# Seven block products for a seventh pair of row tiles, and low parts of the ordinary rows by an adding transfer

## The chip, the cores and the metric

The kernel runs on one core of a Trainium2 chip. The metric is the device time of one execution in microseconds (us). Three executions of the kernel before gave 928.75, 930.30 and 930.32 us; their median is 930.3 us.

## What is computed

A two-layer encoder over 256 tokens of width 1024. Each layer has a feed-forward block, a mixer (two kinds of attention, side by side) and a second feed-forward block, each behind a residual and a layer norm. The change lies in the second matrix product of the feed-forward block, which runs four times:

```python
def swiglu(x, w_in, w_out):                 # D_FF = 2816
    h = x @ w_in
    gate, up = h[..., :D_FF], h[..., D_FF:]
    return (jax.nn.silu(gate) * up) @ w_out
...
for l in range(DEPTH):                      # DEPTH = 2
    x = layer_norm(ALPHA * x + 0.5 * swiglu(x, ffn1_w_in[l], ffn1_w_out[l]), ...)
    x = layer_norm(ALPHA * x + hybrid_mixer(x, ...), ...)
    x = layer_norm(ALPHA * x + 0.5 * swiglu(x, ffn2_w_in[l], ffn2_w_out[l]), ...)
```

## The kernel before

**High and low parts.** Every float32 operand A is split into a high part Ah, rounded to the type fp32r, and a low part Al = A - Ah. A product is three matmuls: Ah·Bh, Ah·Bl and Al·Bh. For a weight row tile of 128x1024 (512 KB), SyncE issues the load into a tile `raw` (L116), ScalarE casts it to `wh` (L118), and VectorE subtracts to get `wl` (L119).

**Buffers and look-ahead.** `raw` has 5 buffers, `wh` and `wl` 9 each, and the general pool `tmp` 7. Buffers of one name are handed out in the order in which the program asks for them. `Weights.get(i)` (L126) asks for the rows ahead, up to nine slots; an ordinary row counts one slot and a pair four. TensorE's instructions run in the order of the program. The other engines' orders are planned at compile time by priority; the splitting work has a lower one (`LATER`).

**The two products of a feed-forward block.** The first makes 22 column tiles of the hidden layer, j = 0 to 21 (`col`, L404, from j = 4 on, mostly two at a time, four weight slots and about 11 us each time). The activations, split, lie in `gs[q]`, q = j // 2. The second product multiplies the 256 tokens (two tiles t = 0, 1) by 22 row tiles k of `w_out`. An ordinary row tile is a `step` (L496): for each t three parts by two column halves, 6 matmuls of 128x512; 12 for both t, and 24 for two row tiles. A pair q in `STR` takes row tiles 2q and 2q+1 as a two by two block matrix and spends seven block products, three matmuls each, 21 in all (`pair`, L507). For it, VectorE forms sums of the weights (L86 to L89: 2 loads in `raw`, a third `raw` for sums, and `t4` in `tmp`), and four splits follow, b, t, a and f (L90 to L93), each a cast (L72) and a subtraction (L73); f is half as wide. The activations' sums are formed in `sums` (L448) when column 2q+1 is done; `f` is a `tmp` tile for a short time, and the results of the first three pairs of `STR` lie in `xp` buffers, those of the others in two `tmp` tiles each, until the pair is through.

**The order of the second product.** `PLAN` gives its first part: six pairs and three ordinary rows, "o o S o S S S S S". Then the four sums of the pair products are folded into the residual (L541 to L550). Then comes the tail of `TAIL` = 7 ordinary rows: first all seven for t = 0 (L552), whose layer norm runs under the following seven for t = 1 (L563). The next stage's rows are loaded and split meanwhile.

**Names in the profile.** Rows have the number in the list of all loads; in the first feed-forward block of layer 0 the pairs are 46 and 48 to 52 (46a and 46b the loads, 46b, 46t, 46a, 46f the splits), the last pair is 52, and TensorE starts the second product at 128.08 us.

Of the kernel before, what the change touches and what calls it, by code (L numbers as in the profile page):

```python
# [9 lines left out]
F32 = mybir.dt.float32  # L10
F32R = mybir.dt.float32r
# [3 lines left out]
ALU = mybir.AluOpType  # L15
# [4 lines left out]
P = 128  # L20
# [4 lines left out]
JT = DFF // P  # L25
# [12 lines left out]
NB = 4  # L38
LATER = 100
WARM = 9  # L40
STR = (3, 4, 5, 6, 7, 8)
PLAN = "o o S o S S S S S"

# [14 lines left out]
class Weights:  # L60
# [15 lines left out]
    def _make_pair(self, i):  # L76
# [16 lines left out]
            (t4,) = self._halves(i, t4, "f")  # L93
        self.made.append((b11, b21, b22, t4, t1, t2, t3))

    def _slots(self, i):
        return 4 if self.srcs[i][0] == "S" else 1

    def _make(self, i):
        nc = self.nc  # L100
        if self.srcs[i][0] == "S":
            return self._make_pair(i)
        raw = self.pool.tile([P, 1024], F32, tag="raw", name=f"raw{i}", bufs=5)
        wh = self.pool.tile([P, 1024], F32R, tag="wh", name=f"wh{i}", bufs=9)
        wl = self.pool.tile([P, 1024], F32R, tag="wl", name=f"wl{i}", bufs=9)

        n = 512 if i < 3 else 1024
        src = self.srcs[i]

        rows = src if isinstance(src, tuple) else (src,)  # L110
        for c in range(0, 1024, n):
            s = slice(c, c + n)
            for q, r in enumerate(rows):
                h = P // len(rows)

                (nc.sync if i or c else nc.scalar).dma_start(raw[q * h : (q + 1) * h, s], r[:, s])  # L116
            with self.tc.high_priority(0 if i < 3 else -LATER):
                nc.scalar.copy(wh[:, s], raw[:, s])  # L118
                nc.vector.tensor_tensor(wl[:, s], raw[:, s], wh[:, s].bitcast(F32), ALU.subtract)  # L119
        self.made.append((wh, wl))  # L120
# [15 lines left out]
def encoder_kernel(  # L136
# [22 lines left out]
    nc = tc.nc  # L159
# [13 lines left out]

    singles = [k for k in range(JT) if k // 2 not in STR]
    singles, tail = singles[: len(singles) - TAIL], singles[len(singles) - TAIL :]
    plan, left, pairs = [], list(singles), list(STR)
    for u in PLAN.split():
        plan.append((u, (left if u == "o" else pairs).pop(0)))
    assert not left and not pairs

    def out_rows(w):
        row = lambda k: w[k * P : (k + 1) * P, :]
        rows = [row(k) if u == "o" else ("S", row(2 * k), row(2 * k + 1)) for u, k in plan]
        return rows + [row(k) for k in tail]

    srcs = []
    for l in range(DEPTH):
        srcs += [f1_b[l, k] for k in range(KT)]
        srcs += [f1_in[l, j, s] for j in range(JT - NB) for s in range(2)]
        srcs += out_rows(f1_out[l])  # L190
        for c in range(3):
            srcs += [m_in[l, c, q] for q in range(4)]
        srcs += [m_in2[l, q] for q in range(2)]
        srcs += [m_in[l, 3, q] for q in range(4)]
        srcs += [m_out[l, k * P : (k + 1) * P, :] for k in range(KT // 2)]

        srcs += [tuple(m_out[l, 512 + 256 * v + HD * n : 512 + 256 * v + HD * (n + 1), :] for v in range(2))
                 for n in range(KT // 2)]
        srcs += [f2_b[l, k] for k in range(KT)]
        srcs += [f2_in[l, j, s] for j in range(JT - NB) for s in range(2)]  # L200
        srcs += out_rows(f2_out[l])
# [5 lines left out]
    xx = cp.tile([P, KT, 2, 2, P], F32R, name="xx")  # L207
# [153 lines left out]
    def ffn(l, n, last=False):  # L361
# [42 lines left out]
        def col(*js, flip=False):  # L404
# [26 lines left out]
            for j, hs, tl, ws in ts:  # L431
                for s in range(2):
                    two(hs, ws, s)
                    nc.scalar.copy(tl[:, s], hs[s][:, 1, :])  # L434
                    dv.tensor_tensor(tl[:, s], hs[s][:, 0, :], tl[:, s], ALU.add)  # L435
                nc.scalar.activation(tl[:, 0], tl[:, 0], AF.Silu)  # L436
                gv = tl[:, 1]
                dv.tensor_tensor(gv, tl[:, 0], gv, ALU.mult)  # L438
                q, jj = divmod(j, 2)
                n = P if q in STR and jj == 0 else SEQ  # L440
                nc.scalar.copy(gs[q][:, jj, 0, 0:n], gv[:, 0:n])  # L441
                dv.tensor_tensor(gs[q][:, jj, 1, 0:n], gv[:, 0:n], gs[q][:, jj, 0, 0:n].bitcast(F32), ALU.subtract)
                if q in STR and jj:
                    sums(q, ts[0][2][:, 1], gv)
# [3 lines left out]
        def sums(q, g0, g1):  # L448

            f = tp.tile([P, 4, P], F32, tag="tmp", name=f"sf_{nm}_{q}")  # L450
            if STR.index(q) < 3:
                s = xp.tile([P, 2, 4, P], F32R, tag="x", name=f"s_{nm}_{q}")
                sh, sl = s[:, 0], s[:, 1]
            else:
                sh, sl = (tp.tile([P, 4, P], F32R, tag="tmp", name=f"s{c}_{nm}_{q}") for c in "hl")
            a11, a21, a12, a22 = g0[:, 0:P], g0[:, P:SEQ], g1[:, 0:P], g1[:, P:SEQ]
            dv.tensor_tensor(f[:, 0], a21, a22, ALU.subtract)
            dv.tensor_tensor(f[:, 1], a11, f[:, 0], ALU.subtract)
            dv.tensor_tensor(f[:, 2], a21, a11, ALU.subtract)
            dv.tensor_tensor(f[:, 3], a12, f[:, 1], ALU.subtract)  # L460
            nc.scalar.copy(sh, f)
            dv.tensor_tensor(sl, f, sh.bitcast(F32), ALU.subtract)
            sm[q] = sh, sl
# [43 lines left out]
        def pair(q, w, first, final):  # L507
            b11, b21, b22, t4, t1, t2, t3 = w
            if first:
                for c in (5, 7, 1, 6):  # L510
                    pp[c] = ps.tile([P, 512], F32, tag="b", name=f"pp_{nm}_{c}")
            sh, sl = sm[q]
            blk = lambda kk, t: [gs[q][:, kk, e, t * P : (t + 1) * P] for e in range(2)]
            smb = lambda c: (sh[:, c], sl[:, c])
            s1, s2, s3, s4 = (smb(c) for c in range(4))
            for o, (ah, al), (bh, bl) in (
                (acc[0][0][1], blk(1, 0), b21),
                (acc[0][1][1], s4, b22),
                (pp[5], s1, t1),
                (pp[7], s3, t3),  # L520
                (pp[1], blk(0, 0), b11),
                (pp[6], s2, t2),
                (acc[1][0][1], blk(1, 1), t4),
            ):
                own = any(o is p for p in pp.values())
                for e, (g, ww) in enumerate(((ah, bh), (ah, bl), (al, bh))):
                    mm(o, g, ww, start=(own and first and e == 0), stop=(own and final and e == 2))  # L527

        for u, k in plan:
            w = W.get(wi)  # L530
            wi += 1
            if u == "S":
                pair(k, w, k == STR[0], k == STR[-1])
            else:
# [3 lines left out]
        c = 0.5 / ALPHA  # L538
# [24 lines left out]
        for n_, (i, cs) in enumerate(todo):  # L563
# [3 lines left out]
            if last and cs is acc[1] and i == TAIL - SPLIT - 1:  # L567
                s, a = acc[1][1][:2]
# [413 lines left out]
```

## Time and profile before

| | |
|---|---|
| median of three executions | 930.3 us (928.75 to 930.32) |
| the profiled execution's own time | 929.28 us |
| its span, first to last instruction | 927.5 us |
| busy: TensorE, VectorE, ScalarE, GpSimd | 919.1, 804.9, 577.8, 17.0 us |
| read from device memory | 174.35 MB |
| granted TensorE clock, mean | 0.997 |

A row of a timeline gives the start in us, the duration in us, the engine, the line, the operation, output and inputs, shapes, the count, and in brackets the idle time ahead of it with what ended it. In a row of a table by windows stand the stretch, its length, then the busy time of TensorE (matmuls), of its weight loads, of VectorE, ScalarE and GpSimd, each with a count, the granted clock, the busy share of the 16 DMA engines and GB/s. Rows of the DMA issues give a count, the size of one and the median us from issue to landing. SPq and DVEq are the instruction queues of SyncE and VectorE.

### The profile page before, as it was taken

The numbers are of one execution on the slowest core, as the hardware profiler recorded it, in microseconds if no ns is written. First come the engines' busy times: TensorE is split into PE (matmuls) and PEld (weight loads), VectorE is DVE, ScalarE is ACT, GpSimd is POOL, SyncE is SP. The second block draws the span as 40 slices with busy tenths as digits, with TensorE's granted clock in tenths as the row PEclk, the third lists the DMA queues.
The fourth block names the chain that finished last, engine by engine and source line by source line (L and its number), as shares of the span: only waits on it lengthen the run. The fifth ranks groups of instructions, "written<-read, shape, count | busy, mean of one in ns | idle before, by whom it ended". The sixth has DMA issues, their size and how long they took to land.

```text
span 927.5 us, 13795 instructions
## 1 busy us (share of the span) xinstructions
PE 919.1 (99%) x4958; PEld 784.9 (85%) x4958; DVE 804.9 (87%) x1388; ACT 577.8 (62%) x982; POOL 17.0 (2%) x27
## 2 busy tenths in 40 slices
PE   9999999999999999999999999999999999999996
PEld 6888888888878888888888888888888888888885
DVE  7898899998987677899986888999988876888997
ACT  5768656546865666656646666664478656666660
POOL 0000000000000000000000000000000000000000
PEclk9999999999999999999999999999999999999998
DMA  8976445774426755545775665466844365665451
GB/s 320 313 265 203 160 137 191 246 260 154 128 90 206 248 182 182 159 136 191 257 262 196 187 192 168 136 231 208 290 112 137 100 236 188 189 192 163 136 205 46
DMA packets 51380, 176.30 MB, mean 190 GB/s; under 512 B 6512, under 2 KB 8304, under 8 KB 51312
## 3 DMA queue, kind: packets, MB, share of 16 engines
q1 hardware_dynamic: 51024, 175.03, 58.0%
q8 instruction: 39, 0.64, 0.3%
q10 hardware_dynamic: 288, 0.39, 0.1%
q14 instruction: 29, 0.24, 0.1%
HBM read 174.35 MB, written 1.05 MB: 189 GB/s over the span
## 4 chain that ended last, share of the span: by engine, by line
PE 98%; DMA 1%; DVE 1%; SPq 0%; issue 0%; ACT 0%; DVEq 0%
PE hg L419 14%; PE hu L419 14%; PE acc L503 12%; PE hb L381 9%; PE hu L424 7%; PE hg L424 7%; PE pp L527 7%; PE acc L527 5%; PE ao L840 5%; PE os L776 1%; PE pj_sq L617 1%; PE pj_sq L619 1%; PE pj_dv L617 1%; PE pj_sq L618 1%; PE pj_dq L618 1%; PE pj_dv L619 1%
## 5 line engine op out<-in xcount | busy, mean ns | idle before, releaser
L119 DVE TENSOR_TENSOR wl<-raw,wh 128x1024 fp32r<-128x1024 f32 (+1 forms) x271 | 325.2, 1207 | 57.0 <-PE hg L424 20.2
L118 ACT CAST wh<-raw 128x1024 fp32r<-128x1024 f32 (+1 forms) x271 | 282.1, 1046 | 99.7 <-PE acc L503 14.8
L419 PE MATMUL hg<-xx,wh 128*128 128x512 f32 x576 | 143.1, 390 | 0.0
L419 PE MATMUL hu<-xx,wh 128*128 128x512 f32 x576 | 142.3, 389 | 0.0
L419 PEld LDWEIGHTS hu<-xx,wh 128*128 128x128 f32 x576 | 108.1, 188 | 22.5
L419 PEld LDWEIGHTS hg<-xx,wh 128*128 128x128 f32 x576 | 106.6, 188 | 21.2
L503 PE MATMUL acc<-wh,g 128*128 128x512 f32 (+1 forms) x326 | 90.5, 386 | 0.0
L424 PE MATMUL hg<-xx,wl 128*128 128x256 f32 x576 | 81.0, 283 | 0.0
L424 PE MATMUL hu<-xx,wl 128*128 128x256 f32 x576 | 80.9, 283 | 0.0
L424 PEld LDWEIGHTS hg<-xx,wl 128*128 128x128 f32 x576 | 75.4, 191 | 1.6
L424 PEld LDWEIGHTS hu<-xx,wl 128*128 128x128 f32 x576 | 74.3, 192 | 0.0
L503 PEld LDWEIGHTS acc<-wh,g 128*128 128x128 f32 x326 | 60.9, 188 | 12.2
L381 PE MATMUL hb<-wh,xx 128*128 128x512 f32 x256 | 69.5, 391 | 0.4 <-ACT wh L118 0.4
L381 PEld LDWEIGHTS hb<-wh,xx 128*128 128x128 f32 x256 | 47.7, 188 | 11.3 <-ACT wh L118 1.6
L503 PE MATMUL acc<-wl,g 128*128 128x512 f32 (+1 forms) x163 | 51.7, 385 | 0.0
L434 ACT COPY tl<-hg 128x256 f32<-128x256 f32 x72 | 26.7, 371 | 30.9 <-PE hg L419 27.4
L434 ACT COPY tl<-hu 128x256 f32<-128x256 f32 x72 | 26.9, 373 | 19.6 <-PE hu L424 16.8
L381 PE MATMUL hb<-wl,xx 128*128 128x512 f32 x128 | 38.9, 390 | 0.0
L441 ACT CAST g<-tl 128x128 fp32r<-128x128 f32 (+1 forms) x72 | 26.7, 371 | 19.2 <-DVE tl L438 18.2
L840 PE MATMUL ao<-wh,xx 128*128 128x512 f32 x128 | 37.0, 398 | 0.0
L503 PEld LDWEIGHTS acc<-wl,g 128*128 128x128 f32 x163 | 30.6, 188 | 6.1
L436 ACT ACTIVATE tl<-tl 128x256 f32<-128x256 f32 x72 | 30.1, 418 | 6.5 <-DVE tl L435 5.7
(1140 smaller groups left out, 1576.3 us busy)
## 6 DMA issues: line engine op xcount, KB each, us to landing
raw<-in_f_in_dram SPq DMA_DIRECT2D x144, 512.0 KB, 4.4
raw<-in_f_out_dram SPq DMA_DIRECT2D x40, 512.0 KB, 4.5
raw<-in_m_in_dram SPq DMA_DIRECT2D x36, 512.0 KB, 4.4
raw<-in_f_b_dram SPq DMA_DIRECT2D x29, 512.0 KB, 4.3
raw<-in_m_out_dram SPq DMA_DIRECT2D x8, 512.0 KB, 5.0
raw<-in_m_out_dram SPq DMA_DIRECT2D x16, 256.0 KB, 4.4
lng<-in_ln_g_dram SPq DMA_DIRECT2D x6, 512.0 KB, 4.9
lnb<-in_ln_b_dram SPq DMA_DIRECT2D x6, 512.0 KB, 6.2
```

What stands on the lines that cost most here:

```text
L118: nc.scalar.copy(wh[:, s], raw[:, s])
L119: nc.vector.tensor_tensor(wl[:, s], raw[:, s], wh[:, s].bitcast(F32), ALU.subtract)
L381: mm(hb[s], xx[:, k, g, t, :], ww[:, 512 * s : 512 * s + 512], start=(k == 0 and e == 0), stop=(k == KT - 1 and e == 2))
L419: mm(hs[s], ws[s][0][:, k * P : (k + 1) * P], xx[:, k], start=(k == 0 and not flip), stop=(k == KT - 1 and flip), skip_group_check=flip)
L424: mm(hs[s][:, 1, :], ws[s][1][:, k * P : (k + 1) * P], xx[:, k, 0], start=(k == 0 and flip), stop=(k == KT - 1 and not flip), skip_group_c ...
L434: nc.scalar.copy(tl[:, s], hs[s][:, 1, :])
L436: nc.scalar.activation(tl[:, 0], tl[:, 0], AF.Silu)
L441: nc.scalar.copy(gs[q][:, jj, 0, 0:n], gv[:, 0:n])
L503: mm(a, g, ww[:, s], start=(k == ka and e == 0), stop=(k == kb and e == 2))
L527: mm(o, g, ww, start=(own and first and e == 0), stop=(own and final and e == 2))
L617: mm(o, xx[:, k, 0, t, :], wh[:, s], start=(k == 0), stop=False)
L840: mm(acc[t][h], xx[:, k, g, t, :], ww[:, s], start=(k == 0 and e == 0), stop=(k == KT - 1 and e == 2))
```

## The change

Row tiles 8 to 21 become seven pairs (q = 4 to 10), rows 0 to 7 stay ordinary: one at the front of the plan, seven in the tail. The ordinary rows of the second product are made in another way (kind "A"): ScalarE casts `raw` to `wh`, then writes -`wh` into `wl`, and GpSimd issues a second transfer of the same 512 KB from device memory that adds to `wl`. The activation sums of the last pair go into the first two slices of `xx`, the block's input, which has been read by then. All other rows are split as before.

```diff
-STR = (3, 4, 5, 6, 7, 8)
-PLAN = "o o S o S S S S S"
+STR = (4, 5, 6, 7, 8, 9, 10)
+PLAN = "o S S S S S S S"
...
+    def _make_added(self, i):
+
+        nc, src = self.nc, self.srcs[i][1]
+        raw = self.pool.tile([P, 1024], F32, tag="raw", name=f"raw{i}", bufs=5)
+        wh = self.pool.tile([P, 1024], F32R, tag="wh", name=f"wh{i}", bufs=9)
+        wl = self.pool.tile([P, 1024], F32R, tag="wl", name=f"wl{i}", bufs=9)
+        nc.sync.dma_start(raw, src)
+        with self.tc.high_priority(-LATER):
+            nc.scalar.copy(wh, raw)
+            nc.scalar.mul(wl, wh.bitcast(F32), -1.0)
+            nc.gpsimd.dma_start(wl, src, accum_op=ALU.add)
+        self.made.append((wh, wl))
...
+        if self.srcs[i][0] == "A":
+            return self._make_added(i)
...
-        rows = [row(k) if u == "o" else ("S", row(2 * k), row(2 * k + 1)) for u, k in plan]
-        return rows + [row(k) for k in tail]
+        rows = [("A", row(k)) if u == "o" else ("S", row(2 * k), row(2 * k + 1)) for u, k in plan]
+        return rows + [("A", row(k)) for k in tail]
...
             if STR.index(q) < 3:
                 s = xp.tile([P, 2, 4, P], F32R, tag="x", name=f"s_{nm}_{q}")
+                sh, sl = s[:, 0], s[:, 1]
+            elif q == JT // 2 - 1:
+                s = xx[:, 0:2].rearrange("p k e t c -> p k (e t) c")
                 sh, sl = s[:, 0], s[:, 1]
             else:
                 sh, sl = (tp.tile([P, 4, P], F32R, tag="tmp", name=f"s{c}_{nm}_{q}") for c in "hl")
```

## The prediction, made before the change was run

> **What bounds the kernel now.** I read the page's busy shares and its chain that ended last, then the chain in order of time over the second product, then VectorE's, ScalarE's, SyncE's and TensorE's timelines there, and the table by windows.
>
> ```profile
> PE 919.1 (99%) x4958; PEld 784.9 (85%) x4958; DVE 804.9 (87%) x1388; ACT 577.8 (62%) x982; POOL 17.0 (2%) x27
> PE 98%; DMA 1%; DVE 1%; SPq 0%; issue 0%; ACT 0%; DVEq 0%
> 128.24 5.44 PE acc L503 x24
> 142.52 2.72 PE pp L527 x12
> 145.24 2.04 PE acc L527 x9
> 128.10:164.80 36.70, 36.70 (x163) 30.40 (x162) 35.86 (x43) 23.61 (x29) 0.00 (x0) 1.00 0.56 186
> 164.80:174.30 9.50, 9.50 (x43) 7.89 (x42) 8.74 (x12) 4.61 (x5) 0.00 (x0) 1.00 0.87 301
> ```
>
> TensorE bounds it: 98% of the chain. Two ordinary rows are 24 matmuls in 5.44 us, 0.2267 us each; a pair is 2.72 + 2.04 = 4.76 us for 21. But TensorE is not alone at the wall. From 128.1 to 164.8, the pairs' part, VectorE is busy 35.86 of 36.70 us. In the first half of the tail the DMA engines are at 0.87 already. So one asks of each operation how early it is, not how long it lasts:
>
> ```profile
> 128.15 1.23 DVE L73 TENSOR_TENSOR wl48b<-raw48b,wh48b 128x1024 fp32r<-128x1024 f32 x1 [0.23 <-ACT wh48b L72]
> 134.38 0.69 DVE L73 TENSOR_TENSOR wl48f<-t,wh48f 128x512 fp32r<-128x512 f32 x1
> 145.31 0.39 PE L527 MATMUL acc<-wl48f,g 128*128 128x512 f32 x1
> 146.37 0.68 DVE L73 TENSOR_TENSOR wl50f<-t,wh50f 128x512 fp32r<-128x512 f32 x1
> 152.79 0.68 DVE L73 TENSOR_TENSOR wl51f<-t,wh51f 128x512 fp32r<-128x512 f32 x1
> 159.20 0.68 DVE L73 TENSOR_TENSOR wl52f<-t,wh52f 128x512 fp32r<-128x512 f32 x1
> 164.35 0.39 PE L527 MATMUL acc<-wl52f,g 128*128 128x512 f32 x1
> 164.80 0.61 PE L503 MATMUL acc<-wh,g 128*128 128x512 f32 x2
> ```
>
> The last split of pair 48 is done at 135.07 and used at 145.31, 10.2 us early; that of pair 52 at 159.88 for 164.35, 4.5 us early. Between pairs VectorE needs 6.41 us (146.37, 152.79, 159.20), TensorE 4.76: each pair in a row eats 1.65 us of the lead.
>
> **The change, part by part.**
>
> *Matmuls.* Per block, two ordinary rows (24) become one pair (21): 3 fewer, 12 in four blocks, 12 x 0.2267 = 2.7 us off the chain. This is all that can be gained; TensorE waits nowhere else for what the change relieves.
>
> *VectorE.* Off go three front rows' subtractions and seven of the tail:
>
> ```profile
> L119 DVE TENSOR_TENSOR wl<-raw,wh 128x1024 fp32r<-128x1024 f32 x265 | 321.1, 1218 | 56.3 <-PE hg L424 20.2 <-ACT wh L118 16.7 <-issue 15.7
> L118 ACT CAST wh<-raw 128x1024 fp32r<-128x1024 f32 x265 | 278.3, 1056 | 94.6 <-PE acc L503 14.8 <-PE hg L419 11.9 <-PE hu L419 10.1
> 113.12 0.69 DVE L462 TENSOR_TENSOR sl<-sf,sh 128x512 fp32r<-128x512 f32 x1 [1.13 <-ACT sh L461]
> 113.84 0.69 DVE L89 TENSOR_TENSOR t<-raw46b,raw46a 128x512 f32<-128x512 f32 x1
> 131.70 0.42 DVE L442 TENSOR_TENSOR g<-tl,g 128x256 fp32r<-128x256 f32 x1
> ```
>
> A subtraction is 1.22 us, so 3.7 us in the pairs' part, against 6.4 us for the added pair there. Worse is a buffer. Six of seven `tmp` tiles hold the sums of three pairs, and `t4` (L89) has only the seventh: pair 46's L89 starts at 113.84, just as the last sums end (113.12 + 0.69). In the new order the sums of q = 10 come after column 21, whose activations are split at 131.70 + 0.42. Four sums, a cast and a subtraction later, about 135 to 136, the second pair's `t4` gets its buffer. Until then both its loads stay occupied, so later pairs' loads start late too. With the third pair's splits done near 141 (L89, f and three splits behind 136) and 6.41 us for each of four more, the seventh pair's last split is done near 141 + 25.6 = 166.7. TensorE would use it at 128.1 + 2.72 + 6 x 4.76 + 4.3 = 163.7. The seventh pair is **3 us late**. Bounds: nothing, if the lead of 4.5 us covers it, to 5.
>
> *The tail's chain.* Today:
>
> ```profile
> 151.80 10.79 SPq L116 DMA_DIRECT2D raw<-in_f_out_dram  x7
> 157.47 0.68 DVE L89 TENSOR_TENSOR t<-raw52b,raw52a 128x512 f32<-128x512 f32 x1
> 158.26 0.62 ACT L72 CAST wh52f<-t 128x512 fp32r<-128x512 f32 x1 [0.63 <-PE pp L527]
> 158.78 2.00 ACT L118 CAST wh<-raw 128x1024 fp32r<-128x1024 f32 x2
> 163.64 0.59 ACT L541 COPY v<-pp 128x512 f32<-128x512 f32 x1
> 165.25 0.62 PE L503 MATMUL acc<-wl,g 128*128 128x512 f32 x2
> 173.41 0.62 PE L503 MATMUL acc<-wl,g 128*128 128x512 f32 x2
> raw<-in_f_out_dram SPq DMA_DIRECT2D x40, 512.0 KB, 4.5
> raw198a<-in_f_out_dram SPq DMA_DIRECT2D x1, 512.0 KB, 3.2
> ```
>
> The tail's seven loads start at 151.80, as pairs free their `raw` tiles. Its casts stand behind the last pair's fourth (wh52f at 158.26, which needs L89 of 157.47), since buffers go out in program order: they start at 158.78, 6.0 us ahead of the tail's first matmul at 164.80. TensorE asks for the first low part at 165.25 and the seventh at 173.41: one every 1.36 us.
>
> In the new chain a row costs ScalarE a cast and a negation. I price both by the cast (two take 2.00 us; the trace has no negation of this size), so 2.0 us a row, 14 for seven, and 0.6 for the copy `v` between them. After that comes the adding transfer. No row shows one. Below stands the fastest load of the same bytes, 3.2 us; above, two loads one after the other, 9.0. I take **5.8**: the median load, 4.5, and 1.3 for reading the second operand at the best rate in the trace:
>
> ```profile
> 12.00:18.00 6.00, 6.00 (x29) 4.94 (x28) 5.14 (x8) 3.76 (x4) 0.00 (x0) 1.00 1.03 406
> q1 hardware_dynamic: 51024, 175.03, 58.0%
> ```
>
> (512 KB at 406 GB/s are 1.29 us.) GpSimd issues the transfers in order, each behind ScalarE's negation of that row; only the layer norm's power (L349), which needs the tail anyway, stands behind them, and its 17 us of work leave it free. On ScalarE the next stage's casts queue behind a negation that waits for its `wl` buffer, and they have slack. The front row is made during the last columns, whose four slots give it 11 us ahead: it costs nothing, and if that cover went, 5.8 less the 1.2 of the subtraction.
>
> The Trainium skill (DMA: Bandwidth & Descriptors, "Anatomy of one DMA — SWDGE (gpsimd) path") prices a transfer issued by GpSimd at about 2.0 us plus its bytes at 436 GB/s, here 3.2 us as an estimate; with it in place of 5.8 the sum below would be 4 x 2.6 = 10 us lower. The page says nothing of the time of an addition, and no run here shows one yet.
>
> With the seventh pair's last split starting 3 us late, at 166.0, its cast starts at 165.1 (today 0.94 ahead of the split) and the tail's casts at 165.7. Row 0 is negated at 167.7 and its low part lands at 173.5. TensorE would begin the tail at 164.1 + 3 = 167.1 and wants it at 167.55: **6 us late**. Row 6 is negated at 165.7 + 14.6 = 180.3 and lands at 186.1 for 175.7: 10.4 late. The DMA engines may be slower still. Beside each add goes a load of the next stage, since each cast frees a `raw` tile; two transfers of 1.29 us make 2.6 us a row, so row 6 lands at 173.5 + 6 x 2.6 = 189.1, **13.4 late**. I take that in the three blocks that have a next stage, and 10.4 in the last, where the loads end. Bounds: if an add takes its engines twice as long and all go at the mean rate (58.0% of 927.5 us for 175.03 MB: 1.61 us per 512 KB), 4.8 us a row, 27 late.
>
> *The clock.*
>
> ```profile
> 918.00:920.50 2.50, 2.34 (x19) 2.10 (x17) 2.20 (x5) 0.00 (x0) 0.00 (x0) 1.00 0.00 0
> 920.50:924.00 3.50, 0.00 (x0) 0.00 (x0) 3.40 (x8) 0.00 (x0) 0.92 (x1) 0.81 0.00 0
> 924.00:927.50 3.50, 0.00 (x0) 0.00 (x0) 0.50 (x2) 0.00 (x0) 0.00 (x0) 0.50 0.43 150
> ```
>
> After the last matmul, at 920.3, the granted clock is at 1.00, then 0.81 on average, then 0.50: it halves about 2 us into idleness. A 6 us wait would do that. Matmuls between the later waits hide it; I add half speed over the first 3.4 us after them, as an estimate of the recovery, 1.7 us a block. Bounds: 0 to 3.4.
>
> *Sum.* Three blocks of 3 + 13.4 + 1.7 = 18.1 and one of 3 + 10.4 + 1.7 = 15.1 are 69.4; less 2.7 is 66.7. On the profiled execution's own 929.28 us (its span of 927.5 and 1.8 around it) that is **996 us**. The median, 930.3, is 1.0 above that execution, well inside what I don't know.
>
> **The rivals.**
>
> *Nothing waits.* The relieved VectorE keeps its lead, and the adds run ahead unseen: 929.3 - 2.7 = 926.6, faster. For it: VectorE loses 40 subtractions of 1.22 us and gains only four pairs of 6.4, and ScalarE has 38% of the span free. Against it: row 6 needs 14.6 us of ScalarE and 5.8 of transfer, so the casts would have to start 20.4 - 8.6 = 11.8 us ahead of the tail's first matmul; today they start 6.0 ahead, behind a last pair that comes no earlier. That is the point from which it decides. 7%.
>
> *Only the tail waits.* The pairs keep their lead, casts start 6.0 us ahead as today, and the engines move both transfers: row 6 lands 14.4 us after the tail's start and is due at 8.6, so 5.8 late. 4 x 5.8 - 2.7 gives 950; with 3.2 us for the add, 940. For it: buffers and loads free up earlier with casts alone. Against it: 6.41 against 4.76, seven times running. 11%.
>
> *The adds are starved.* GpSimd writes its transfers' descriptors while VectorE is busy 98% of the time. If each add waits out one VectorE operation more, 1.2 us, on its first row, 4 x 1.2 gives 1001. The Trainium skill (SBUF — State Buffer, "Who interferes with whom") lets VectorE lock GpSimd out in two-port modes only, which a `tensor_tensor` hasn't got; so by that page this should not occur, and the trace has no transfer of GpSimd's to tell. 3%.
>
> *It doesn't do what it says.* If the planner puts the adds so late that they cancel the matmuls saved and no more, the time is within 0.2% of 930. 2%.
>
> **How the numbers follow.** The forecast, late pairs and a late tail, has 77%: 996 us. Its own spread is large, as the add's engine time is unknown: with 4.8 us a row, 5 for the pairs and 1.7 for the clock, four blocks give 134 - 2.7 and 1060 us. The range goes from 940, the lower price of "only the tail waits", to 1050, just short of that corner. Left out are 926.6, the case of no change and the corner, together under 2 in 10. About 0.2% is what a measurement of this kernel can tell from no change. Faster: 7%. Same: 2%. Slower: 91%.
>
> **What would show it.** Matmul count down by 12. The pairs' first matmuls waiting for `wl` from L73 in the last two or three pairs, 3 us a block. In the tail, TensorE's idle time put down to the add into `wl`, one long wait at the first row and shorter ones at each row after; two ScalarE operations a row, back to back; windows with a granted clock below 1 in the tail; DMA share near 1 there. It is wrong if an add lands in far under 3 us, if the tail's casts start 12 us ahead of it, or if the second pair's L89 starts before the last activation sums are done and VectorE never idles.

## The result, and the profile after

The changed kernel takes 1039.6 us (median of four, 1037.4 to 1042.3) against 930.2 us (928.8 to 930.3) for the one before on the same chip: a ratio of 1.118 [1.115, 1.122], 109 us slower. The profiled execution has a span of 1040.5 us, 113.0 more than before.

The page of the changed kernel: busy shares, granted clock, DMA queues, the chain that ended last, two groups of TensorE's and GpSimd's, and the landing of the adds.

```profile
PE 957.8 (92%) x4946; PEld 792.3 (76%) x4946; DVE 794.3 (76%) x1400; ACT 611.1 (59%) x1025; POOL 44.7 (4%) x59
PEclk9999998799999999998699999988999999999989
q1 hardware_dynamic: 51024, 175.03, 51.3%
q0 software_dynamic: 4608, 16.78, 8.3%
PE 70%; DVE 14%; DMA 8%; issue 4%; ACT 4%; POOL 0%; DVEq 0%; ACTq 0%; POOLq 0%
L521 PE MATMUL acc<-wl,g 128*128 128x512 f32 (+1 forms) x131 | 53.9, 482 | 65.3 <-DMA wl<-in_f_out_dram 65.3
L106 POOL DMA_DIRECT2D wl<-in_f_out_dram x32 | 27.6, 864 | 670.4 <-ACT wl L105 460.6
wl<-in_f_out_dram POOLq DMA_DIRECT2D x32, 512.0 KB, 12.0
```

The 12 matmuls are gone (4958 to 4946), and nothing else became shorter. TensorE's part of the chain falls from 98% to 70%. VectorE has 14% of it, the DMA engines 8%, and 65.3 us of TensorE's idleness end with a low part that lands from the adding transfer. TensorE's busy time grows although it does less: its clock dips four times, once in each tail.

The first block in order of time, the changed kernel (its seven pairs are 45 to 51): VectorE's, ScalarE's and GpSimd's timelines, then TensorE's weight loads, two of the last pair and some of those that first use a low part in the tail.

```profile
134.71 0.69 DVE L480 TENSOR_TENSOR xx<-sf,xx 128x512 fp32r<-128x512 f32 x1 [0.69 <-ACT xx L479]
135.44 0.69 DVE L89 TENSOR_TENSOR t<-raw46b,raw46a 128x512 f32<-128x512 f32 x1
...
166.09 1.22 DVE L73 TENSOR_TENSOR wl51a<-raw51a,wh51a 128x1024 fp32r<-128x1024 f32 x1
...
166.81 1.99 ACT L104 CAST wh<-raw 128x1024 fp32r<-128x1024 f32 x2
168.70 0.58 ACT L559 COPY v<-pp 128x512 f32<-128x512 f32 x1
169.18 1.06 ACT L105 ACTIVATE wl<-wh 128x1024 fp32r<-128x1024 f32 x1
...
170.55 0.86 POOL L106 DMA_DIRECT2D wl<-in_f_out_dram  x1 [60.87 <-ACT wl L105]
...
181.99 0.86 POOL L106 DMA_DIRECT2D wl<-in_f_out_dram  x1 [1.16 <-ACT wl L105]
...
163.89 0.19 PEld L545 LDWEIGHTS acc<-wl51b,g 128*128 128x128 f32 x1 [1.02 <-DVE wl51b L73]
...
167.36 0.19 PEld L545 LDWEIGHTS pp<-wl51a,g 128*128 128x128 f32 x1 [0.51 <-DVE wl51a L73]
...
179.15 0.50 PEld L521 LDWEIGHTS acc<-wl,g 128*128 128x128 f32 x2 [9.64 <-DMA wl<-in_f_out_dram]
...
198.88 0.30 PEld L521 LDWEIGHTS acc<-wl,g 128*128 128x128 f32 x2 [2.59 <-DMA wl<-in_f_out_dram]
202.68 0.30 PEld L521 LDWEIGHTS acc<-wl,g 128*128 128x128 f32 x2 [2.57 <-DMA wl<-in_f_out_dram]
```

The pairs first. TensorE starts the second product at 127.93 and the tail at 169.30, 41.4 us for 36.0 us of matmuls (one row of 2.72 and seven pairs of 4.76): 5.4 us late, in short waits for VectorE's splits in the last three pairs. Then the tail. GpSimd issues the first add at 170.55, as soon as the row is negated, and TensorE gets it at 179.15, 8.6 us later, after an idle time of 9.6 us. The next ones come some 3.8 us apart (198.88, 202.68), where a row of matmuls needs 1.36. So t = 0 takes 34.6 us (169.3 to 203.9) instead of 9.5.

The table by windows over that tail, and the same weight loads and a row by windows in the last block, where no next stage is loaded alongside:

```profile
169.30:180.00 10.70, 1.50 (x5) 0.95 (x4) 5.35 (x8) 10.70 (x12) 4.28 (x6) 0.69 1.02 295
180.00:200.00 20.00, 12.37 (x34) 7.76 (x34) 2.45 (x2) 2.74 (x3) 1.69 (x2) 0.74 1.06 275
200.00:212.50 12.50, 10.36 (x39) 8.08 (x38) 7.94 (x13) 4.21 (x4) 0.93 (x1) 0.86 0.21 69
```

```profile
1007.48 0.50 PEld L521 LDWEIGHTS acc<-wl,g 128*128 128x128 f32 x2 [9.15 <-DMA wl<-in_f_out_dram]
...
1019.88 0.30 PEld L521 LDWEIGHTS acc<-wl,g 128*128 128x128 f32 x2 [1.23 <-DMA wl<-in_f_out_dram]
1022.33 0.30 PEld L521 LDWEIGHTS acc<-wl,g 128*128 128x128 f32 x2 [1.21 <-DMA wl<-in_f_out_dram]
...
1007.50:1022.30 14.80, 11.91 (x36) 8.23 (x36) 0.00 (x0) 1.98 (x3) 1.70 (x2) 0.81 0.97 192
```

The DMA engines are full (share 1.02 and 1.06) and yet move 295 and 275 GB/s, against the 406 GB/s at a share of 1.03 quoted ahead. VectorE and ScalarE are nearly idle from 180 to 200. In the last block the rows come 2.45 us apart, with the engines' share at 0.97, VectorE idle and ScalarE nearly so: this is what one add of 512 KB takes of the engines when it is alone. The other 1.35 of the 3.8 would then be the next stage's load beside it.

The four second products, from first to last matmul, take 88.0, 87.7, 87.8 and 76.4 us, where the kernel before has 57.3, 56.8, 56.9 and 56.0. The differences add up to 112.9 of the 113.0 us: the whole loss is there.

### The profile page after: what moved, and what is told of

Its sections match the earlier page's. It is cut to its first block, busy times and chain, and to the rows that moved or that the text cites. A ratio compares the mean times of both kernels' runs of the same rounds, so it can differ in the third digit from the quotient of the medians.

```text
span 1040.5 us, 13872 instructions
## 1 busy us (share of the span) xinstructions
PE 957.8 (92%) x4946; PEld 792.3 (76%) x4946; DVE 794.3 (76%) x1400; ACT 611.1 (59%) x1025; POOL 44.7 (4%) x59
## 4 chain that ended last, share of the span: by engine, by line
PE 70%; DVE 14%; DMA 8%; issue 4%; ACT 4%; POOL 0%; DVEq 0%; ACTq 0%; POOLq 0%
PE hg L434 12%; PE hu L434 12%; PE hb L396 8%; DMA wl<-in_f_out_dram 7%; PE hu L439 7%; PE hg L439 7%; PE acc L521 4%; PE ao L858 4%; ACT wh L104 2%; ACT wl L105 1%; DVE t L89 1%; DMA raw<-in_m_in_dram 1%; PE os L794 1%; PE pj_sq L637 1%; PE pj_sq L635 1%
## 5 line engine op out<-in xcount | busy, mean ns | idle before, releaser
L134 DVE TENSOR_TENSOR wl<-raw,wh 128x1024 fp32r<-128x1024 f32 (+1 forms) x231 | 277.3, 1206 | 88.2 <-ACT wh L133 46.2
L133 ACT CAST wh<-raw 128x1024 fp32r<-128x1024 f32 (+1 forms) x231 | 240.1, 1045 | 142.2 <-PE acc L521 68.6
L521 PE MATMUL acc<-wl,g 128*128 128x512 f32 (+1 forms) x131 | 53.9, 482 | 65.3 <-DMA wl<-in_f_out_dram 65.3
L521 PEld LDWEIGHTS acc<-wl,g 128*128 128x128 f32 x131 | 26.9, 226 | 83.4 <-DMA wl<-in_f_out_dram 80.2
L521 PE MATMUL acc<-wh,g 128*128 128x512 f32 (+1 forms) x262 | 86.9, 447 | 0.0
L521 PEld LDWEIGHTS acc<-wh,g 128*128 128x128 f32 x262 | 58.5, 225 | 14.0
L106 POOL DMA_DIRECT2D wl<-in_f_out_dram x32 | 27.6, 864 | 670.4 <-ACT wl L105 460.6
L396 PEld LDWEIGHTS hb<-wh,xx 128*128 128x128 f32 x256 | 48.3, 190 | 10.4 <-ACT wh L133 0.5
L358 DVE SCALAR_TENSOR_TENSOR x<-acc,x 128x512 f32<-128x512 f32 (+1 forms) x13 | 8.1, 645 | 56.7 <-PE acc L521 56.7
```

The lines of the kernel that those rows point to most:

```text
L106: nc.gpsimd.dma_start(wl, src, accum_op=ALU.add)
L396: mm(hb[s], xx[:, k, g, t, :], ww[:, 512 * s : 512 * s + 512], start=(k == 0 and e == 0), stop=(k == KT - 1 and e == 2))
L521: mm(a, g, ww[:, s], start=(k == ka and e == 0), stop=(k == kb and e == 2))
```

## The experiments

**Theory T**: the adds cost more than the pairs, by the time that they occupy the DMA engines and by their late start; the pairs are late because of VectorE and the one free `tmp` tile. The rivals put the main loss on the seventh pair (P), on GpSimd's issuing (G), on ScalarE's two operations a row (A), or on a fixed cost of each add (F). All times are medians of four runs (six for e12), beside runs of the kernel before on the same chip, 929.5 to 930.3 us.

### Which of the two parts?

Seven pairs, with every ordinary row split on VectorE (e1), and the converse, the old plan with the adds (e2):

```diff
# e1, in out_rows
-    rows = [("A", row(k)) if u == "o" else ...
-    return rows + [("A", row(k)) for k in tail]
+    rows = [row(k) if u == "o" else ...
+    return rows + [row(k) for k in tail]
# e2
-STR = (4, 5, 6, 7, 8, 9, 10)
-PLAN = "o S S S S S S S"
+STR = (3, 4, 5, 6, 7, 8)
+PLAN = "o o S o S S S S S"
```

> Edit: the seven pairs stay, but all eight ordinary rows get their low parts from VectorE's subtraction again (no negation, no adding transfer). Theory T (the adds are the larger part of the loss: their landing time and 2.46 us of all DMA engines each; the pairs are about 5.4 us late per block): about 955 us, range 945 to 970, with the first tail row of the first block still about 5 us late and no wait over 2 us in the tail. Rival P (the seventh pair, VectorE's work, is the main loss): 1010 us or more. Rival N (pairs cost nothing): 930 or less.

> Edit: the plan of the kernel before (six pairs, three front rows, six old places of the pairs) with the adding transfer for all its ordinary rows. Theory T: the pairs' 5 us a block are saved and the tail's waits stay; about 1011 us (995 to 1025). Rival P (the seventh pair is the main loss): 960 or less.

e1: 960.5 us, 1.033 [1.031, 1.035]. e2: 1013.3 us, 1.089 [1.084, 1.093]. Both lie where theory T had them; P and N fall. The adds cost 79 us with seven pairs (1039.6 - 960.5) and 83 with six (1013.3 - 930.3), the seventh pair 31 without adds and 26 with them; so the two parts nearly add (31 + 83 = 114 against 109). In e2 the pairs are as before (141.1 to 165.1), and the tail takes from 164.9 to 209.8, 44.9 us against 20.6.

The table by windows over the first block's second product, the pairs' part and the tail, in e1:

```profile
127.70:169.10 41.40, 39.06 (x160) 29.01 (x159) 39.95 (x55) 23.60 (x30) 0.00 (x0) 1.00 0.47 158
169.10:192.80 23.70, 21.83 (x94) 16.29 (x93) 23.44 (x32) 14.01 (x15) 0.91 (x1) 1.00 0.75 250
```

VectorE is busy 39.95 + 23.44 = 63.4 of 65.1 us, and TensorE has 56.6 us of matmuls (57.3 before, less 3 of 0.2267). So with seven pairs split on VectorE the stage is VectorE's. That is why someone would want its subtractions elsewhere, but the place chosen costs more.

### Is the front row's add free?

e4 is e1 with the adding transfer for the front row alone; e12 is the old plan with adds for its three front rows.

```diff
# e4: e1 with this line as in the changed kernel
-    rows = [row(k) if u == "o" else ...
+    rows = [("A", row(k)) if u == "o" else ...
# e12: e4 with STR and PLAN as in e2
```

> Edit: as e1, but the one front row of each block keeps negation and adding transfer; the seven tail rows are split on VectorE. Theory T: the front row's add is issued long before it is used and hidden, so within 4 us of e1 (about 955). Rival (an add costs the other loads of the stage wherever it stands): 8 us or more above e1.

> Edit: the plan of the kernel before (six pairs), with negation and adding transfer for its front rows alone; the tail's rows are split on VectorE. Theory T: the front rows' adds are issued in the first product and hidden, and VectorE's relief buys nothing because TensorE does not wait there: 927 to 933 us, no difference from before. Rival D (adds take DMA time from other loads wherever they stand): 940 or more.

e4 takes 961.0 us, 0.5 more than e1: hidden, as expected. e12 takes 933.5, 1.005 [1.003, 1.006], just over the range expected and a real loss, though a small one. In the first block its second product lasts 56.8 us, no longer than before; in the second 59.9 against 56.8 and in the third 57.8 against 56.8. There TensorE waits for VectorE, in the tail and behind it (waits by engine, e12):

```profile
PE tr_y L342 <- DVE x L370: 1.6, 2, 1.0
PE acc L521 <- DVE wl L134: 0.7, 1, 0.7
```

No wait is for an add, and D, which has 940 or more, falls. What makes the 4 us was not tried: it may be the order in which the planner has put VectorE's work, or the adds' traffic.

### What in an add costs: the addition, the issue or the negation?

e3 makes the transfer a plain one; e9 adds only half of the columns; e6 replaces the negation by a zeroing on GpSimd.

```diff
# e3
-            nc.gpsimd.dma_start(wl, src, accum_op=ALU.add)
+            nc.gpsimd.dma_start(wl, src)
# e9
+            nc.gpsimd.dma_start(wl[:, 0:512], src[:, 0:512], accum_op=ALU.add)
# e6
-            nc.scalar.mul(wl, wh.bitcast(F32), -1.0)
+            nc.gpsimd.memset(wl.bitcast(F32), 0.0)
```

> Edit: GpSimd's transfer of an ordinary row into wl is a plain copy instead of an accumulating one; queue, size, order and waits stay. The low part is then the whole row, so the output is not the reference's. Theory T (the accumulation itself occupies the DMA engines, 2.46 us a row against 1.3): the tail's low parts land about 2.6 us apart beside the next block's loads and 1.3 to 1.9 apart in the last block, the first about 6 us after its issue, total about 994 us (980 to 1005). Rival G (GpSimd's issuing and writing of descriptors, 0.86 us an instruction and what follows, sets the pace): spacing stays at 3.8 and 2.5 us, total 1035 or more.

> Edit: the adding transfer takes only the first 512 of the 1024 columns (256 KB instead of 512 KB); the other half of the low part stays the negated high part, so the output is not the reference's. Theory T (the price of an add is time of the DMA engines, by the byte: 2.46 us for 512 KB, so 1.23, and 1.35 for the load beside it): low parts about 2.6 us apart beside loads, 1.2 to 1.9 in the last block, total 985 to 1010. Rival F (a fixed cost of each accumulating transfer): 3.5 us or more apart, total 1030 or more.

> Edit: ScalarE's negated copy is left out; GpSimd zeroes wl ahead of its adding transfer instead, so the low part is the whole row and the output is not the reference's. ScalarE then has one operation a row, about 1 us, instead of two. Theory T (the transfers set the row rate): spacing stays at 3.8 us, the first transfer starts at most 1 us earlier, or later if the zeroing is slow; total 1030 to 1045. Rival A (ScalarE's two operations a row, 2 us, and its place in the order set the tail): the rows come at least 1 us closer, total 1010 or less.

e3 takes 1003.4 us, 1.079 [1.078, 1.081], and e9 1005.5 us, 1.082 [1.081, 1.084]. The DMA queue and weight loads of the tail in e3, then in e9:

```profile
q0 software_dynamic: 4608, 16.78, 4.7%
...
177.52 0.50 PEld L521 LDWEIGHTS acc<-wl,g 128*128 128x128 f32 x2 [8.12 <-DMA wl<-in_f_out_dram]
187.88 0.30 PEld L521 LDWEIGHTS acc<-wl,g 128*128 128x128 f32 x2 [1.33 <-DMA wl<-in_f_out_dram]
190.44 0.30 PEld L521 LDWEIGHTS acc<-wl,g 128*128 128x128 f32 x2 [1.34 <-DMA wl<-in_f_out_dram]
```

```profile
q0 software_dynamic: 4608, 8.39, 4.8%
...
178.41 0.50 PEld L521 LDWEIGHTS acc<-wl,g 128*128 128x128 f32 x2 [8.62 <-ACT wh L104]
191.37 0.30 PEld L521 LDWEIGHTS acc<-wl,g 128*128 128x128 f32 x2 [1.33 <-issue]
194.03 0.30 PEld L521 LDWEIGHTS acc<-wl,g 128*128 128x128 f32 x2 [1.43 <-issue]
```

The plain transfer of the same size, on the same queue, brings the rows down from 3.8 to 2.6 us apart; so does an add of half the size. Both say the same: an add takes engine time mostly by the byte, nearly twice that of a copy. The queue's line agrees, as share times span over 32 transfers: 2.70 us for an add of 512 KB, 1.47 for a plain one, 1.50 for an add of 256 KB, so that at most some 0.3 us of an add don't go by the byte. (In e9 the waits are put down to ScalarE or to "issue" from the first row on. TensorE had multiplied by the same row's `wh` just before; read as waits for the landing, they fit the spacing.) G and F fall. GpSimd's timeline in the changed kernel speaks against G too: the last of the seven adds is issued at 181.99, 20.7 us before its low part is used (202.68). e3's total is at the upper end of its range, since the first row still comes late: 177.52 for an issue at 170.44, 7.1 us against the add's 8.6. That one wait, 8.1 us, is about half of the 15 by which t = 0 is longer in e3's first block.

e6 takes 1008.1 us, 1.084 [1.083, 1.086], 31.6 less than the changed kernel. Theory T missed it, and the total lies where rival A had it, though only half of A's reason is borne out. Of e6, GpSimd's timeline, ScalarE's, and TensorE's weight loads:

```profile
159.71 0.86 POOL L106 DMA_DIRECT2D wl<-in_f_out_dram  x1
...
174.57 1.04 ACT L104 CAST wh<-raw 128x1024 fp32r<-128x1024 f32 x1 [3.03 <-DMA raw<-in_f_out_dram]
178.44 1.04 ACT L104 CAST wh<-raw 128x1024 fp32r<-128x1024 f32 x1 [2.83 <-DMA raw<-in_f_out_dram]
...
169.63 0.42 PEld L521 LDWEIGHTS acc<-wl,g 128*128 128x128 f32 x2
...
187.49 0.42 PEld L521 LDWEIGHTS acc<-wl,g 128*128 128x128 f32 x2
191.24 0.41 PEld L521 LDWEIGHTS acc<-wl,g 128*128 128x128 f32 x2
```

Without a cast to wait for, GpSimd issues the tail's adds from 159.71 on, 10.8 us earlier than in the changed kernel, and the first row is used at 169.63 with no wait. That is what was gained, and here A is right: it is ScalarE's work ahead of the first add that makes it late. But ScalarE does not set the pace. The later rows come as far apart as ever (187.49 to 191.24, 3.75 us), though ScalarE has one operation a row and sits idle about 3 us ahead of each. It now waits for the loads of `raw`, which share the engines with the adds. Two transfers a row set the pace, whichever of them is last. Of the 79 us that the adds cost, 36 go with the addition itself (e3) and 32 with the start behind ScalarE (e6); the two were not taken out together.

### How many added rows?

e11 adds only the last three rows of the tail; the four ahead are split on VectorE.

```diff
# e11: e1 with
-    return rows + [row(k) for k in tail]
+    return rows + [("A", row(k)) if k in tail[-3:] else row(k) for k in tail]
```

> Edit: seven pairs; of the ordinary rows only the last three of the tail keep negation and adding transfer, the others are split on VectorE as in e1. Theory T (an add costs a landing of 8 to 9 us after ScalarE's cast and then 3.8 us for each further one, and the four rows ahead do not cover it): the first of the three is late by some 4 us, the last by some 10 us a block, total 985 to 1005. Rival H (four rows ahead hide the landing, and VectorE is relieved of three splits): 960 or less.

1006.7 us, 1.083 [1.082, 1.085], a little over T's range; H falls. Of e11, ScalarE's and GpSimd's timelines, and the weight loads in the tail:

```profile
172.12 1.05 ACT L104 CAST wh<-raw 128x1024 fp32r<-128x1024 f32 x1 [0.78 <-DMA raw<-in_f_out_dram]
...
174.58 1.02 POOL L106 DMA_DIRECT2D wl<-in_f_out_dram  x1 [172.37 <-ACT wl L105]
...
174.12 0.30 PEld L521 LDWEIGHTS acc<-wl,g 128*128 128x128 f32 x2 [0.51 <-DVE wl L134]
184.60 0.50 PEld L521 LDWEIGHTS acc<-wl,g 128*128 128x128 f32 x2 [9.25 <-DMA wl<-in_f_out_dram]
188.44 0.50 PEld L521 LDWEIGHTS acc<-wl,g 128*128 128x128 f32 x2 [1.64 <-DMA wl<-in_f_out_dram]
192.23 0.50 PEld L521 LDWEIGHTS acc<-wl,g 128*128 128x128 f32 x2 [1.58 <-DMA wl<-in_f_out_dram]
```

Four rows ahead cover nothing: the add of the fifth is issued at 174.58, just when TensorE wants it, because its cast comes as late as its `raw` load. The first wait is nearly as long as with seven rows (9.25 us against 9.64). Three adds cost 11.6 us a block over e1 ((1006.7 - 960.5) / 4) and seven 19.8 (79.1 / 4), so by a straight line through the two, an estimate, each further row costs 2.1 and the first about 7.4.

### GpSimd's own subtraction instead

```diff
# e7, in _make_added
-            nc.scalar.mul(wl, wh.bitcast(F32), -1.0)
-            nc.gpsimd.dma_start(wl, src, accum_op=ALU.add)
+            nc.gpsimd.tensor_tensor(wl, raw, wh.bitcast(F32), ALU.subtract)
```

> Edit: seven pairs; the low parts of the eight ordinary rows come from a subtraction on GpSimd in place of negation and adding transfer. Theory T: GpSimd's subtraction of 1024 columns takes some 2 to 4 us, longer than a row of matmuls (1.36 us), so the tail waits 1 to 2.5 us a row: 965 to 1020 us. Rival (the tail's loss came from the ScalarE order, which stays): 1030 or more.

985.3 us, 1.059 [1.058, 1.061], within T's range. The groups of e7 by line:

```profile
L105 POOL TENSOR_TENSOR wl<-raw,wh 128x1024 fp32r<-128x1024 f32 x32 | 85.3, 2695 | 627.6 <-ACT wh L104 396.5
L520 PE MATMUL acc<-wl,g 128*128 128x512 f32 (+1 forms) x131 | 45.2, 410 | 26.6 <-POOL wl L105 26.6
```

GpSimd takes 2.70 us for what takes VectorE 1.22. That is faster than 3.8 and slower than a row of matmuls, and so is the time: between the changed kernel and e1.

### Why are the pairs late?

The prediction named one `tmp` tile. e5 takes the last sums' temporary out of that ring; e8 and e10 also move two rows, or one, from the tail to the front.

```diff
# e5: e1, and in sums()
+            if q == JT // 2 - 1:
+                f = ps.tile([P, 4, P], F32, tag="b", name=f"sf_{nm}_{q}")
+            else:
                 f = tp.tile([P, 4, P], F32, tag="tmp", name=f"sf_{nm}_{q}")
# e8: e5 with PLAN = "o o o S S S S S S S", TAIL = 5
# e10: e5 with PLAN = "o o S S S S S S S", TAIL = 6
```

> Edit: as e1, and the temporary of the last pair's sums lies in a PSUM bank instead of the ring of tmp tiles, so that the second pair's t4 no longer waits for a tmp tile until the sums of row pair 10 are done. Theory T (that ring accounts for most of what the pairs lose): about 949 us (942 to 955), 5 us or more below e1, and t4 of the second pair before 134 us in the first block. Rival V (VectorE's 6.41 us a pair alone makes the pairs late): within 3 us of e1.

> Edit: as e5, with two of the ordinary rows moved from the tail to the front (three front rows, tail of five), seven pairs, all splits on VectorE. Theory T: the longer front gives VectorE 5 us more ahead of the first pair, so the pairs are hardly late: 930 to 942 us, below e5. Rival V (VectorE's total work in the second product is over TensorE's, so a shift of rows only moves the wait): within 3 us of e5.

> Edit: as e8, with one ordinary row moved from the tail to the front instead of two (two front rows, tail of six). Theory V (VectorE's work in the second product is over TensorE's, and a shift of rows only moves the wait between the pairs, the tail's splits and the first layer norm): 944 to 954 us, within 6 us of e8 on either side and slower than before. Rival B (one shift balances both ends): 935 or less.

e5 takes 957.9 us, 1.030 [1.028, 1.031]: 2.6 us below e1, not 11. VectorE's timeline in e5, then TensorE's (45 is the first pair), and the same wait added up over the four blocks:

```profile
128.39 0.68 DVE L89 TENSOR_TENSOR t<-raw46b,raw46a 128x512 f32<-128x512 f32 x1
...
136.96 0.51 PE L548 MATMUL pp<-wh45a,s 128*128 128x512 f32 x1 [2.41 <-DVE xx L483]
```

```profile
PE pp L548 <- DVE xx L483: 9.7, 4, 2.4
```

The buffer did what was said of it: the second pair's `t4` comes at 128.39 instead of after 135. But the pairs' part hardly moves: from the first pair to the tail, seven pairs take 37.7 us (130.98 to 168.64) against 38.7 in e1, where 33.3 are matmuls. VectorE's 39.95 us of work there are the same, with hardly a gap in either run, and its last split of the pairs ends at 167.03 instead of 167.70. The 2.4 us a block that TensorE now waits are the edit's own. The temporary holds one of the eight buffers of the PSUM ring until the sums of q = 10 are through (L483); by the order of the program's requests, the first pair's last `pp` product gets that same buffer. This wait hides little: in the last pair, split `a` is done at 166.44 and used at 166.82, so without it TensorE would have stood before VectorE's splits instead. Theory T falls in this part, and V holds.

e8 takes 949.5 us, 1.021 [1.019, 1.023], e10 959.1, 1.031 [1.030, 1.033]. Both missed their range on the slow side. In e8 the pairs are on time (135.85 to 169.31, 33.5 us), and the wait stands elsewhere (waits of e8):

```profile
PE tr_y L342 <- DVE x L370: 11.4, 3, 3.8
```

With five rows the tail's second half no longer covers the first layer norm. e10 has short waits in all three places, the pairs, the tail's splits and the layer norm. V's claim that a shift only moves the wait holds for e10; e8's gain of 8 us over e5 speaks against its strict form. Why two rows moved gain 8 us where one gains none was not tried. B falls with e10. No version here beats the kernel before, and none could by much: seven pairs save TensorE 2.7 us in all.

## Why the prediction was right in direction and low in size

The path was as forecast, late pairs and then a tail that waits for its adds. The time lies in the stated range, though, only because that range reached up to just short of the corner of slow adds; the forecast of 996 us itself is 44 short, and nearly all of that lies in the tail, in the price of an add.

**Matmuls**: 12 fewer, as said, and nothing else gained.

**The pairs**: 5.4 us late a block, not 3, a little over the bound of 5. The signs were right (`t4` at 135.44, short waits for L73 in the last three pairs), and the last pair's cast came at 166.28, 1.2 us after the 165.1 forecast. The reason was half right: e5 freed the `tmp` tile and got back 1.0 us of 5.4 in the first block. What decides is VectorE's work, 6.41 us a pair against 4.76 for TensorE. Two steps make up most of the 2.4 us that the forecast lacks. VectorE was through with the third pair at 142.24, not 141. And in the last pair TensorE waits for split `a` (done at 167.31, used at 167.36), not for `f`, from which the forecast reckoned: that one was done at 167.91 and used at 168.85, 0.9 later.

**The front row** is free, as said (e4).

**The first low part** came 9.6 us late, not 6. ScalarE did two casts and the copy `v` ahead of the first negation, so that the add left 1.25 us into the tail, where 0.6 had been reckoned. The rest is the landing: 8.6 us instead of 5.8, within the bounds of 3.2 and 9.0. Only 1.5 of the 8.6 go with the addition, since the plain transfer in e3 took 7.1. The 3.2 us worked out from the Trainium skill (DMA: Bandwidth & Descriptors, "Anatomy of one DMA — SWDGE (gpsimd) path") for a transfer issued by GpSimd do not hold here: even the plain one took 7.1 us, with the engines' share at 1.04.

**The row rate** is the term that failed. The prediction gave an add the engine time of a plain transfer, 1.29 us at the best rate, and so 2.6 us a row with a load beside it. The runs show 2.45 for the add alone and 3.8 with a load. t = 0 ends 25 us late instead of 13.4 in the three blocks with a next stage, and 16 instead of 10.4 in the last. Of the 11.7 us a block between, 3.6 come with the first low part (9.6 late instead of 6) and 8 with the rate. Half of the corner was the case: the add takes its engines about twice as long. Its other half, the mean rate of 1.61 us, was not; three times the best rate's 1.29 make 3.9 us a row, and 3.8 were measured, where the corner had 4.8. The mechanism, two transfers a row on full engines, was right.

**The clock**: the term of 1.7 us a block was too large. What is lost behind the waits is 0.9 us in the first block (203.9 to 215.9 against 174.3 to 185.4) and none in the last; most of the slow matmuls lie between waits for the adds, where by the row rate they cost nothing. The clock also fell later than the 2 us that the forecast read from the kernel before: TensorE goes idle at 169.95, and the granted clock is 1.00 from 170 to 172, 0.84 from 172 to 174 and 0.50 from there, so it halved some 3.4 us into the wait.

Term by term, actual less forecast: pairs 4 x 2.35 = 9.4, rows 3 x 11.7 + 5.6 = 40.7, clock 3 x (0.9 - 1.7) - 1.7 = -4.1. Together 46.0 us; the span of 1040.5 less the forecast's (996 - 1.8 = 994.2) is 46.3.

**The rivals**: "nothing waits" fails at its own point of decision, since the casts began 2.5 us ahead of the tail (166.81 for 169.30), not 11.8. "Only the tail waits" is e2's case in the plan of before: it cost far more than the 950 reckoned, for the same mis-sized add. The starved adds are not seen: GpSimd issued the first 0.3 us after its negation, and its issuing instruction took 0.86 us, and two of them at 1008.83, with VectorE idle, took 1.80.

## What to carry to other kernels

Before work is moved off an engine, ask what price the new resource charges per byte in the very stretch where it lands: here the subtraction of 1.22 us on VectorE became 2.45 us of all DMA engines where they were already at 0.87. An operation that starts only after a cast cannot be hidden by its own short duration; it needs the whole landing as lead, as the front row had and the tail had not. And a wait that is put down to one buffer should first be checked against the busy sum of the engine that fills it: e5 freed the buffer, and VectorE's last split came 0.7 us earlier.

## What the runs showed of the hardware that was not expected

- An accumulating transfer occupies the DMA engines about 1.8 times as long as a copy of the same bytes: 2.70 against 1.47 us per 512 KB by the queue's share, 3.8 against 2.6 us a row with a load beside it. It goes nearly by the byte: 1.50 us for 256 KB (e9).
- GpSimd's instruction for it lasts 0.86 us (864 ns over 32). For the plain transfer in e3 it lasted 0.53.
- GpSimd's subtraction of 128x1024 took 2.70 us, 2.2 times VectorE's 1.22, and that with VectorE at work beside it.
- The granted clock was 0.69 in the stretch of the 9.6 us wait and still 0.74 in the 20 us behind it, in which short waits went on (the windows of the changed kernel, above). In e11 it was back at 1.00 within some 8 us of the last wait at 192.23, by its table of windows:

```profile
180.00:200.00 20.00, 13.62 (x38) 9.96 (x39) 6.22 (x10) 2.84 (x4) 1.14 (x2) 0.60 0.63 171
200.00:215.00 15.00, 15.00 (x76) 12.56 (x76) 14.98 (x22) 6.29 (x9) 1.06 (x2) 1.00 0.66 206
```
